# Modulation products in four column quarters of the array, and the square of the decay on ScalarE

## The chip, the cores and the metric

The kernel runs on one core of a Trainium2 chip. The metric is device time in microseconds: the median of three runs before was 2331.62 us (2330.88 to 2336.09). The profiled execution took 2334.22 us in all, and its span, from the first to the last instruction, 2332.4 us.

## The reference, cut to what matters

Two layers of a hybrid mixer are run for 1024 latent and 256 context tokens of 1024 channels. Each layer is modulated by a conditioning vector, one for each of the two token groups:

```python
mod = jnp.dot(jax.nn.silu(cvec), p['w_ada']) + p['b_ada']   # 1024 -> 3072
shift, scale, gate = jnp.split(mod[:, None, :], 3, axis=-1)
h = rmsnorm(x, p['norm_g']) * (1.0 + scale) + shift
...                                   # attention, Hyena and RG-LRU heads from h
a = jnp.exp(log_a)                    # the RG-LRU's decay
b = jnp.sqrt(-jnp.expm1(2.0 * log_a)) * (i * xf)
...
x_new = x + gate * out                # out: the output projection
```

`mod` is a product of two rows (the two conditioning vectors) with a 1024 x 3072 matrix, once a layer, all in float32. `expm1(2 log_a)` comes from the decay: it is a*a - 1.

## The kernel before, in words

Channels lie on the 128 partitions, in eight tiles of 128, and tokens run along the free dimension, in chunks of 512, 512 and 256. Large projections are done with weights and activations split into two float16 halves (`proj`, L680; `out_acc`, L1316), three products for each pair of tiles.

The modulation is done with the conditioning vectors as the stationary operand (128 x 2) and the matrix as the moving one (128 x 512), so that 512 outputs take eight products, one for each tile of the 1024 contracted channels, added up in two partitions of one PSUM tile. A float32 product stands in the trace as two passes. Those two rows of 512 are then copied to SBUF by VectorE, turned by four transposes of TensorE into columns (128 x 2 each), and added to the bias into `modv`. Two generators do this:

- `ada()` makes shift and scale of layer 0 at the start of the program: four rows of 512 (products on L473, copies on L476, transposes on L479). The 16 matrix tiles of 128 x 1024 (`wa`, 512 KB each) are loaded in the order that the string `ORD` gives, mixed with the eight input tiles `xs`. They have eight buffers (tag `h`), so that the second eight wait until the first eight have been multiplied. `ada_in(0)` then makes `sh_t` and `sc_t`, without which the first normalised tile (`make_h`) can't be made. `make_h` also needs `first`, the inverse norm that `FirstSquares` makes on TensorE, ScalarE and VectorE.
- `ada_rest(l, o0)` makes the other rows in steps (products on L499, copies on L502, transposes on L506): two rows of layer 0 (its gate) beside the RG-LRU of layer 0, and six rows of layer 1 beside the output projection of layer 0. Four tiles of 256 KB are loaded in one step (tag `bn`, four buffers, which other lines use too) and multiplied in the next.

`weave` mixes the steps of such generators into a main loop, each at a rate of its own, and so gives the order of the source. The program's order on each engine is not that order to the letter: a list scheduler issues the earliest instruction of the source that it takes to be ready, by its own estimates of durations. At run time every engine's order is fixed. All DMAs are issued in order from SyncE's queue.

In `lru_post`, for each of four channel tiles and two directions in a layer, the decay `a` comes from ScalarE (Exp). GpSimd multiplies it by itself into `a2`, and VectorE uses `a2` in a `scalar_tensor_tensor` that gives a*a - 1 times a factor. Another one, on `ti`, stands just before it on VectorE. Calls to ScalarE show as L155, to VectorE as L149 and L152, and GpSimd's products as L152, since helpers record them.

Of the kernel before, what the change touches and what calls it, by code (L numbers as in the profile page):

```python
# [10 lines left out]
F32 = mybir.dt.float32  # L11
F16 = mybir.dt.float16
AF = mybir.ActivationFunctionType
ALU = mybir.AluOpType
AX = mybir.AxisListType
ADD, SUB, MUL, MAX, MIN = ALU.add, ALU.subtract, ALU.mult, ALU.max, ALU.min

P = 128
# [4 lines left out]
T = NL + NP  # L23
# [5 lines left out]
KT = 8  # L29
# [24 lines left out]
PRM = {}  # L54
# [57 lines left out]
def hybrid_step(ctx, tc, xT, cT, w_ada, w_in, w_out, prm, fpk, w1, w2, w3, decay, ck, cv, wlru,  # L112
# [3 lines left out]
    cp = ctx.enter_context(tc.tile_pool(name="cp", bufs=1))  # L116
# [5 lines left out]
    V, A, G, PE = nc.vector, nc.scalar, nc.gpsimd, nc.tensor  # L122
# [4 lines left out]
    def nm(s):  # L127
        uid[0] += 1
        return f"{s}_{uid[0]}"


    def S(tag, shape=(P, W5), dt=F32):
        return sp.tile(list(shape), dt, tag=tag, name=nm(tag), bufs=BUFS[tag])
# [4 lines left out]
    def B(tag, shape=(P, 512), dt=F32):  # L138
        return S(tag, shape, dt)

    def PS(tag, shape=(P, 512)):
        tag = PTAG[tag]
        return ps.tile(list(shape), F32, tag=tag, name=nm(tag), bufs=PTAG["n" + tag])

    def load(dst, src):
        return nc.sync.dma_start(dst, src)

    def stt(out, a, s, b, o0=MUL, o1=ADD, eng=None):
        return (eng or V).scalar_tensor_tensor(out, a, s, b, o0, o1)  # L149

    def tt(out, a, b, op, eng=None):
        (eng or V).tensor_tensor(out, a, b, op)  # L152

    def act(out, a, f, scale=1.0, bias=0.0):
        A.activation(out, a, f, bias=bias, scale=scale)  # L155
# [30 lines left out]
    modv = cp.tile([P, DEPTH, 24, 2], F32, name="modv")  # L186
# [19 lines left out]
    def pv(l, name, i=0):  # L206
        o, n = PRM[name]
        return pr[:, l, o + i:o + i + 1]
# [247 lines left out]
                    load((Hl, Hp)[kind][l, hf, q], h)  # L456
                    yield

    silu_c = cp.tile([P, KT, 2], F32, name="silu_c")

    def ada():

        sc = silu_c
        th = sm.tile([P, KT, 2], F32, name="th_c")
        act(th, cT_t, AF.Tanh, scale=0.5)
        V.tensor_scalar(th, th, 0.5, 0.5, MUL, ADD)
        tt(sc, th, cT_t, MUL)
        for o in (0, 8):
            p = [PS("m" if o else "s") for _ in range(2)]
            for k in range(KT):  # L470
                wt = wa[o + k]
                for i, pi in enumerate(p):
                    PE.matmul(pi[:2], sc[:, k], wt[:, 512 * i:512 * i + 512], start=(k == 0), stop=(k == KT - 1))  # L473
            for i, pi in enumerate(p):
                row = B("ba")
                V.tensor_copy(row[:2, :512], pi[:2])  # L476
                pt = PS("o")
                for j in range(4):
                    PE.transpose(pt[:, 2 * j:2 * j + 2], row[:2, P * j:P * j + P], ident[:2, :2])  # L479
                q = o + 4 * i  # L480
                b = pr[:, 0, PRM["b_ada"][0] + q:PRM["b_ada"][0] + q + 4]
                tt(modv[:, 0, q:q + 4], pt[:, :8].rearrange("p (a b) -> p a b", b=2),
                   b[:, :, None].to_broadcast([P, 4, 2]), ADD)
            if o:
                ada_in(0)
            yield

    def ada_rest(l, o0=0):

        for o in range(o0, 24, 4):  # L490
            p = PS("s")
            for k0 in range(0, KT, 4):
                raws = []
                for k in range(k0, k0 + 4):
                    raws.append(B("bn"))
                    load(raws[-1], w_ada[l, k, :, P * o:P * o + 512])
                yield
                for k, raw in enumerate(raws, k0):
                    PE.matmul(p[:2], silu_c[:, k], raw, start=(k == 0), stop=(k == KT - 1))  # L499
                yield  # L500
            row = B("bn")
            V.tensor_copy(row[:2, :512], p[:2])  # L502
            yield
            pt = PS("s")
            for j in range(4):
                PE.transpose(pt[:, 2 * j:2 * j + 2], row[:2, P * j:P * j + P], ident[:2, :2])  # L506
            b = pr[:, l, PRM["b_ada"][0] + o:PRM["b_ada"][0] + o + 4]
            tt(modv[:, l, o:o + 4], pt[:, :8].rearrange("p (a b) -> p a b", b=2),
               b[:, :, None].to_broadcast([P, 4, 2]), ADD)
            if o == 12:  # L510
                ada_in(l)
            yield
        V.tensor_scalar(gt_t[:, l], modv[:, l, 16:24], 1.0 / SW, None, MUL)

    def ada_in(l):
        V.tensor_scalar(sh_t[:, l], modv[:, l, 0:8], SH, None, MUL)
        g = pvs(l, "norm_g")

        V.tensor_scalar(sc_t[:, l], modv[:, l, 8:16], 1.0, -0.5 * SH, ADD, MUL)
        tt(sc_t[:, l], sc_t[:, l], g[:, :, None].to_broadcast([P, 8, 2]), MUL)  # L520
# [195 lines left out]
    def conv(u, taps, bias):  # L716

        t = S("a")
        for a, b, o in ((0, NL, 0), (NL, T, GAP - NL)):
            act(t[:, a:b], u[:, a + o:b + o], AF.Identity, scale=taps[0], bias=bias)  # L720
            for j in range(1, len(taps)):
                stt(t[:, a:b], u[:, a + o + j:b + o + j], taps[j], t[:, a:b])
        return t

    def park(i, m):

        for c0, n in CH:
            t = B("ba", (P, 2, 512), F16)
            act(t[:, 0, :n], m[:, c0:c0 + n], AF.Copy)
            tt(t[:, 1, :n], m[:, c0:c0 + n], t[:, 0, :n], SUB, G)  # L730
            load(Md[i, :, :, c0:c0 + n], t[:, :, :n])
# [33 lines left out]
    def lru_post(l, i, out):  # L765
        u, gate = out[i]
        xc = conv(u, [pv(l, "lw", 4 * i + j) for j in range(4)], pv(l, "lb", i))
        wr, wt = B("ld", (P, 4, P)), B("ld", (P, 2, 4, P), F16)
        load(wr, wlru[l, i])
        act(wt[:, 0], wr, AF.Copy, scale=SW)  # L770
        stt(wt[:, 1], wr, SW, wt[:, 0], MUL, SUB)
        x2 = S("a", (P, 2, W5), F16)
        act(x2[:, 0, :T], xc[:, :T], AF.Copy)
        tt(x2[:, 1, :T], xc[:, :T], x2[:, 0, :T], SUB, ENG[XL])
        yield
        st = []
        for d in range(2):
            ta, ti = S("a"), S("a")
            for c0, n in CH:
                for z, dst, bo_ in ((0, ta, 4 * d + i), (1, ti, 8 + 4 * d + i)):  # L780
                    p = PS("s")
                    for j, (a, b) in enumerate(((0, 0), (0, 1), (1, 0))):
                        PE.matmul(p[:, :n], wt[:, a, 2 * d + z], x2[:, b, c0:c0 + n], start=(j == 0), stop=(j == 2))
                    act(dst[:, c0:c0 + n], p[:, :n], AF.Tanh, scale=0.5 / SW, bias=hba[:, l, bo_:bo_ + 1])
                yield
            s_, n_ = lr_sp[:, l, 0, 4 * d + i:4 * d + i + 1], lr_sp[:, l, 1, 4 * d + i:4 * d + i + 1]
            a = S("a")

            act(a[:, :T], ta[:, :T], AF.Exp, scale=s_, bias=s_)
            act(ta[:, :T], ta[:, :T], AF.Tanh, scale=n_, bias=n_)  # L790
            stt(ti[:, :T], ti[:, :T], 1.0, xc[:, :T], ADD, MUL)
            a2 = S("a")
            tt(a2[:, :T], a[:, :T], a[:, :T], MUL, G)
            stt(ta[:, :T], a2[:, :T], 1.0, ta[:, :T], ADD, MUL)
            st.append((a, ta, ti))
            yield
        for d, (a, ta, ti) in enumerate(st):
            act(ta[:, :T], ta[:, :T], AF.Sqrt, scale=0.25)
        ys = []
        for d, (a, ta, ti) in enumerate(st):  # L800
            tt(ti[:, :T], ti[:, :T], ta[:, :T], MUL, ENG[LE[d]])
            h0 = pv(l, "h0", 4 * d + i)
            L, Q = slice(0, NL), slice(NL, T)
            if d:
                L, Q = slice(NL - 1, None, -1), slice(T - 1, NL - 1, -1)
            V.tensor_tensor_scan(ta[:, L], a[:, L], ti[:, L], h0, MUL, ADD)
            V.tensor_tensor_scan(ta[:, Q], a[:, Q], ti[:, Q], 0.0, MUL, ADD)
            e = NL if d else T - 1
            load(newh[l, d, i], ta[:, e:e + 1])
            ys.append(ta)  # L810
            yield
        m = ys[0]
        tt(m[:, :T], ys[0][:, :T], ys[1][:, :T], ADD, ENG[LE[2]])
        stt(m[:, :T], m[:, :T], GS, gate[:, :T], MUL, MUL)
        yield
        park(4 + i, m)
        yield
# [569 lines left out]
    xs, wa = [], []  # L1387
    for c in ORD:
        if c == "x":
            i = len(xs)  # L1390
            xs.append(S("f" if i < 4 else "a"))
            load(xs[i][:, :T], xT[i])
        elif c == "c":
            ident = const("ident", [P, P], ident_in)
            pr = const("pr", [P, DEPTH, NPRM], prm)
            ones = const("ones", [P, P], ones_h)
        else:
            i = len(wa)
# [237 lines left out]
```

## Time and profile before

| | value |
|---|---|
| median of three runs | 2331.62 us |
| profiled execution: time, span | 2334.22 us, 2332.4 us |
| TensorE (PE) busy | 2103.2 us, 90% |
| VectorE (DVE) busy | 1730.1 us, 74% |
| ScalarE (ACT) busy | 1232.3 us, 53% |
| GpSimd (POOL) busy | 806.5 us, 35% |
| mean granted clock of TensorE | 0.967 |

Busy time of TensorE is that of pipelined instructions: in a row of equal matmuls the distance from start to start is shorter than the duration of one, and it is the distance that counts. PEld is the loading of stationary operands, which overlaps the matmuls. "Idle before <-" names what ended the idle time before an instruction. DVE, ACT, POOL and SP stand for VectorE, ScalarE, GpSimd and SyncE.

### The profile page before, as it was taken

To read this page: it belongs to the slowest core of one execution; us is meant where nothing else is said; L and a number is where in the kernel's file an instruction comes from. 1 tells how busy PE (TensorE), PEld (TensorE's weight loads), DVE (VectorE), ACT (ScalarE), POOL (GpSimd) and SP (SyncE) were. 2 spreads that over 40 slices of the span, in tenths; PEclk is the share of its full clock that TensorE was granted. 3 is DMA by queue.
4 is the path that set the end of the run, shared out by engine and by line. 5 is a ranking of instruction groups with operands and counts; after the bars stand their busy time and mean duration, and the time that the engine had idled before them with its cause. 6 is when DMAs were issued, how large, how long until landed. Compare 5 with 4: busy or idle time off the path is not lost. (4 is left out here: it accounts for less than half of the span.)

```text
span 2332.4 us, 38033 instructions
## 1 busy us (share of the span) xinstructions
PE 2103.2 (90%) x14288; PEld 1238.6 (53%) x14288; DVE 1730.1 (74%) x2765; ACT 1232.3 (53%) x2157; POOL 806.5 (35%) x746
## 2 busy tenths in 40 slices
PE   8787889989998999999998899999899898999997
PEld 2344435546544566676444444455555556666674
DVE  6987887487769888875757877766774998777547
ACT  6765755334333477676342677634433427566562
POOL 4332142123503365565212321131440316444450
PEclk9899989999999999999999999999999999999999
DMA  7314215234214432112475122223431334111114
GB/s 272 123 37 123 76 56 133 63 109 133 84 39 137 126 117 67 56 56 93 151 230 178 46 53 43 56 69 93 135 94 55 113 103 148 53 57 57 46 45 153
DMA packets 154696, 226.10 MB, mean 97 GB/s; under 512 B 22148, under 2 KB 74541, under 8 KB 154512
## 3 DMA queue, kind: packets, MB, share of 16 engines
q1 hardware_dynamic: 154512, 223.67, 31.6%
q8 instruction: 112, 1.84, 0.3%
q14 instruction: 72, 0.59, 0.1%
HBM read 170.73 MB, written 49.03 MB: 94 GB/s over the span
## 5 line engine op out<-in xcount | busy, mean ns | idle before, releaser
L680 PE MATMUL acc<-h,wh 128*128 128x512 f16 (+1 forms) x3264 | 864.0, 351 | 38.4 <-DVE f L149 17.1
L680 PE MATMUL acc<-h,wl 128*128 128x512 f16 (+1 forms) x1632 | 571.8, 350 | 0.0
L680 PEld LDWEIGHTS <-wh 128*128 128x128 f16 x3264 | 324.1, 99 | 311.7 <-issue 69.6
L152 POOL TENSOR_TENSOR y<-by,y 128x512 f16<-128x512 f32 x272 | 318.0, 1188 | 229.8 <-issue 138.1
L680 PEld LDWEIGHTS <-wl 128*128 128x128 f16 x1632 | 162.4, 99 | 162.6 <-issue 38.0
L155 ACT ACTIVATE f<-acc 128x512 f32<-128x512 f32 (+1 forms) x204 | 105.2, 519 | 264.9 <-PE acc L680 263.1
L1316 PE MATMUL acc<-h,wh 128*128 128x512 f16 (+1 forms) x768 | 199.3, 344 | 0.0
L155 ACT ACTIVATE by<-s 128x512 f32<-128x512 f32 x208 | 135.1, 649 | 110.3 <-PE s L1197 109.5
L1170 DVE TENSOR_REDUCE mxl<-m 128x1 f32<-128x512 f32 x288 | 186.3, 680 | 8.7 <-PE m L1169 8.6
L149 DVE SCALAR_TENSOR_TENSOR a<-f,pr,a 128x1024 f32<-128x1024 f32 (+1 forms) x144 | 147.9, 1045 | 60.1 <-ACT a L155 57.7
L152 DVE TENSOR_TENSOR y<-by,y 128x512 f16<-128x512 f32 x128 | 121.2, 947 | 66.5 <-ACT y L155 62.9
L155 ACT ACTIVATE wh<-wr 128x512 f16<-128x512 f32 x184 | 113.4, 626 | 94.8 <-PE acc L1316 47.8
L1223 PE MATMUL o<-va,y 128*128 128x130 f16 x1600 | 160.4, 220 | 1.8 <-DVE f L149 1.7
L1224 PE MATMUL o<-va,y 128*128 128x65 f16 x1600 | 155.3, 193 | 7.1 <-POOL y L152 6.0
L1316 PEld LDWEIGHTS <-wh 128*128 128x128 f16 x1152 | 108.8, 98 | 88.9 <-issue 10.6
L1224 PEld LDWEIGHTS <-y 128*128 128x128 f16 x1600 | 140.9, 98 | 23.2 <-POOL y L152 8.8
L1223 PEld LDWEIGHTS <-y 128*128 128x128 f16 x1600 | 142.2, 97 | 12.7 <-issue 7.8
L370 PE MATMUL m<-y,ld 128*128 128x256 f16 x960 | 122.7, 277 | 26.4 <-ACT y L155 14.9
L152 DVE TENSOR_TENSOR y<-y,y 128x256 f32<-128x256 f32 (+4 forms) x160 | 127.6, 826 | 13.0 <-ACT y L155 13.0
L149 DVE SCALAR_TENSOR_TENSOR wl<-wr,wh 128x512 f16<-128x512 f32 x168 | 130.2, 784 | 8.7 <-ACT wh L155 7.8
L155 ACT ACTIVATE y<-s 128x512 f16<-128x512 f32 x208 | 136.0, 654 | 0.0
L1169 PE MATMUL m<-k,a 128*128 128x512 f16 x288 | 110.8, 385 | 24.9 <-DVE mxl L1170 23.7
(209 smaller groups left out, 4147.3 us busy)
## 6 DMA issues: line engine op xcount, KB each, us to landing
wr<-in_w_in SPq DMA_DIRECT2D x136, 256.0 KB
bn<-in_w_ada SPq DMA_DIRECT2D x64, 256.0 KB
wr<-in_w_out SPq DMA_DIRECT2D x48, 256.0 KB
ld<-in_fhl SPq DMA_DIRECT2D x56, 192.0 KB
h<-Md SPq DMA_DIRECT2D x16, 640.0 KB
h<-in_w_ada SPq DMA_DIRECT2D x16, 512.0 KB
Md<-ba SPq DMA_DIRECT2D x32, 256.0 KB
Hl<-by SPq DMA_DIRECT2D x32, 256.0 KB
```

What stands on the lines that cost most here:

```text
L149: return (eng or V).scalar_tensor_tensor(out, a, s, b, o0, o1)
L152: (eng or V).tensor_tensor(out, a, b, op)
L155: A.activation(out, a, f, bias=bias, scale=scale)
L370: PE.matmul(x[:, o], cn[:, y, c], hl[:, z, g], start=(k == 0 and j == 0), stop=(k == 1 and j == 2))
L680: PE.matmul(acc[:, :n], w[k // 4][wi][:, P * (k % 4):P * (k % 4) + P], h[k][:, x, c0:c0 + n], start=(k == 0 and j == 0), stop=(k == KT - 1 ...
L1169: PE.matmul(p, lhs, k1[g][:, 512 * c:512 * c + 512], start=True, stop=True)
L1170: V.tensor_reduce(mxl[:, 8 * e + qt, c:c + 1], p, AX.X, MAX)
L1223: PE.matmul(o[:, qt], p[:, 0], va[g][:, s0 + s], start=(s == 0), stop=False)
L1224: PE.matmul(o[:, qt, 0], p[:, 1], va[g][:, s0 + s, 0], start=False, stop=(s == ns - 1))
L1316: PE.matmul(acc[:, :n], wt[:, cs], mix[k][:, x, c0:c0 + n], start=(i == 0 and j == 0), stop=(i == len(ks) - 1 and j == 2))
```

## The change

The stationary operand `silu_c` gets 32 columns for each contraction tile, two with the vectors and thirty of zeros. The product of contraction tile k is put into the column quarter k mod 4 of the array (`tile_position`), and so into 32 partitions of its own of the PSUM tile, where tiles k and k + 4 add up. The row of 128 partitions is copied whole, and instead of four transposes four products with a 0/1 matrix `pick` (128 x 2, made from the identity) both turn it and add the four quarters. In `ada()` the products of four contraction tiles stand together in the source, first those of one PSUM tile and then those of the other. In `ada_rest` the step between the copy and the transposes is gone. In `lru_post` the square of the decay is an activation of ScalarE.

```diff
--- before.py
+++ after.py
@@ -456,11 +456,28 @@
                     load((Hl, Hp)[kind][l, hf, q], h)
                     yield
 
-    silu_c = cp.tile([P, KT, 2], F32, name="silu_c")
+    silu_c = cp.tile([P, KT, 32], F32, name="silu_c")
+    pick = cp.tile([P, 2], F32, name="pick")
+
+    def ada_row(p, row, pt, l, q):
+
+        V.tensor_copy(row, p)
+        for j in range(4):
+            PE.matmul(pt[:, 2 * j:2 * j + 2], row[:, P * j:P * j + P], pick, start=True, stop=True)
+        b = pr[:, l, PRM["b_ada"][0] + q:PRM["b_ada"][0] + q + 4]
+        tt(modv[:, l, q:q + 4], pt[:, :8].rearrange("p (a b) -> p a b", b=2),
+           b[:, :, None].to_broadcast([P, 4, 2]), ADD)
+
+    def ada_mm(p, w, k):
+
+        j = 32 * (k % 4)
+        PE.matmul(p[j:j + 32], silu_c[:, k], w, start=(k < 4), stop=(k >= KT - 4), tile_position=(0, j))
 
     def ada():
 
-        sc = silu_c
+        sc = silu_c[:, :, 0:2]
+        V.memset(silu_c, 0.0)
+        V.tensor_reduce(pick, ident.rearrange("p (j b) -> p b j", j=4)[:, 0:2], AX.X, ADD)
         th = sm.tile([P, KT, 2], F32, name="th_c")
         act(th, cT_t, AF.Tanh, scale=0.5)
         V.tensor_scalar(th, th, 0.5, 0.5, MUL, ADD)
@@ -468,19 +485,13 @@
         for o in (0, 8):
             p = [PS("m" if o else "s") for _ in range(2)]
             for k in range(KT):
-                wt = wa[o + k]
+                if k % 4 < 3:
+                    continue
                 for i, pi in enumerate(p):
-                    PE.matmul(pi[:2], sc[:, k], wt[:, 512 * i:512 * i + 512], start=(k == 0), stop=(k == KT - 1))
+                    for k4 in range(k - 3, k + 1):
+                        ada_mm(pi, wa[o + k4][:, 512 * i:512 * i + 512], k4)
             for i, pi in enumerate(p):
-                row = B("ba")
-                V.tensor_copy(row[:2, :512], pi[:2])
-                pt = PS("o")
-                for j in range(4):
-                    PE.transpose(pt[:, 2 * j:2 * j + 2], row[:2, P * j:P * j + P], ident[:2, :2])
-                q = o + 4 * i
-                b = pr[:, 0, PRM["b_ada"][0] + q:PRM["b_ada"][0] + q + 4]
-                tt(modv[:, 0, q:q + 4], pt[:, :8].rearrange("p (a b) -> p a b", b=2),
-                   b[:, :, None].to_broadcast([P, 4, 2]), ADD)
+                ada_row(pi, B("ba")[:, :512], PS("o"), 0, o + 4 * i)
             if o:
                 ada_in(0)
             yield
@@ -496,17 +507,9 @@
                     load(raws[-1], w_ada[l, k, :, P * o:P * o + 512])
                 yield
                 for k, raw in enumerate(raws, k0):
-                    PE.matmul(p[:2], silu_c[:, k], raw, start=(k == 0), stop=(k == KT - 1))
+                    ada_mm(p, raw, k)
                 yield
-            row = B("bn")
-            V.tensor_copy(row[:2, :512], p[:2])
-            yield
-            pt = PS("s")
-            for j in range(4):
-                PE.transpose(pt[:, 2 * j:2 * j + 2], row[:2, P * j:P * j + P], ident[:2, :2])
-            b = pr[:, l, PRM["b_ada"][0] + o:PRM["b_ada"][0] + o + 4]
-            tt(modv[:, l, o:o + 4], pt[:, :8].rearrange("p (a b) -> p a b", b=2),
-               b[:, :, None].to_broadcast([P, 4, 2]), ADD)
+            ada_row(p, B("bn"), PS("s"), l, o)
             if o == 12:
                 ada_in(l)
             yield
@@ -790,7 +793,7 @@
             act(ta[:, :T], ta[:, :T], AF.Tanh, scale=n_, bias=n_)
             stt(ti[:, :T], ti[:, :T], 1.0, xc[:, :T], ADD, MUL)
             a2 = S("a")
-            tt(a2[:, :T], a[:, :T], a[:, :T], MUL, G)
+            act(a2[:, :T], a[:, :T], AF.Square)
             stt(ta[:, :T], a2[:, :T], 1.0, ta[:, :T], ADD, MUL)
             st.append((a, ta, ti))
             yield
```

## Rows read from the trace of the kernel before

**Rows 1.** Page, part 1: busy us (share of the span) xinstructions

```profile
PE 2103.2 (90%) x14288; PEld 1238.6 (53%) x14288; DVE 1730.1 (74%) x2765; ACT 1232.3 (53%) x2157; POOL 806.5 (35%) x746
```

**Rows 2.** Busy time by stretch, us from the start; columns in the first line

```profile
core 0: us, PE busy (x) PEld busy (x) DVE busy (x) ACT busy (x) POOL busy (x), PEclk, DMA share, GB/s
14.00:64.00 50.00, 47.43 (x111) 12.15 (x110) 36.68 (x59) 34.55 (x61) 19.07 (x19) 0.97 0.66 252
...
130.00:420.00 290.00, 243.36 (x1283) 128.32 (x1283) 229.92 (x250) 167.92 (x236) 82.80 (x68) 0.91 0.32 83
1080.00:1250.00 170.00, 156.50 (x866) 73.68 (x863) 111.88 (x173) 61.77 (x110) 42.93 (x25) 0.99 0.55 178
1300.00:1530.00 230.00, 206.28 (x1053) 105.70 (x1052) 175.97 (x162) 155.56 (x226) 53.54 (x62) 0.94 0.21 45
```

**Rows 3.** Readers of silu_c: count, min/median/max ns, first and last start, form

```profile
L499 PEld LDWEIGHTS s<-bn,silu_c x128: 80/84/129, 166.3 to 1240.3; 128*2 128x2 f32 x128
L499 PE MATMUL s<-bn,silu_c x128: 591/592/1061, 166.3 to 1240.8; 128*2 128x512 f32 x128
...
L473 PE MATMUL s<-h,silu_c x32: 591/592/1057, 14.0 to 43.2; 128*2 128x512 f32 x32
...
L473 PE MATMUL m<-h,silu_c x32: 591/592/593, 44.0 to 62.6; 128*2 128x512 f32 x32
```

**Rows 4.** PE timeline, 54 to 69 us: start, length, operation, count, [idle before]

```profile
54.49 8.74 PE L473 MATMUL m<-h,silu_c 128*2 128x512 f32 x20
63.16 0.41 PE L479 MATMUL o<-ident,ba 2*128 2x2 f32 x4
...
68.13 1.01 PE L680 MATMUL acc<-h,wh 128*128 128x512 f16 x2 [3.65 <-ACT h L155]
```

**Rows 5.** DVE timeline, 57 to 66 us

```profile
57.28 0.69 DVE L149 SCALAR_TENSOR_TENSOR by<-bn,bn 128x512 f32<-128x512 f32 x1
...
65.90 0.16 DVE L152 TENSOR_TENSOR sc_t<-sc_t,pr 128x16 f32<-128x16 f32 x1
```

**Rows 6.** PE timeline, 1102 to 1107 us

```profile
1102.62 0.38 PE L1316 MATMUL acc<-a,wl 128*128 128x512 f16 x1
1102.92 3.59 PE L499 MATMUL s<-bn,silu_c 128*2 128x512 f32 x8
1106.45 0.39 PE L1316 MATMUL acc<-h,wh 128*128 128x256 f16 x2
```

**Rows 7.** Line L579 (ones product of FirstSquares): weight loads, columns as in Rows 3

```profile
L579 PEld LDWEIGHTS acc<-bn,ones x24: 186/190/337, 27.3 to 54.0; 128*128 128x128 f32 x24
```

**Rows 8.** Waits, PEld, 1080 to 1250 us: us in total, times, longest

```profile
PEld s L499 <- DMA bn<-in_w_ada: 11.9, 16, 2.3
```

**Rows 9.** Timelines of POOL and DVE at 212 us, of DVE at 1364

```profile
212.20 2.32 POOL L152 TENSOR_TENSOR a<-a 128x1280 f32<-128x1280 f32 x1 [10.22 <-ACT a L155]
...
212.51 4.75 DVE L149 SCALAR_TENSOR_TENSOR a<-a,a 128x1280 f32<-128x1280 f32 x2 [3.84 <-ACT a L155]
...
1364.62 1.47 DVE L149 SCALAR_TENSOR_TENSOR a<-a,a 128x1280 f32<-128x1280 f32 x1
```

**Rows 10.** DVE groups, 130:420 and 1300:1560: busy us, mean ns | idle before

```profile
L149 DVE SCALAR_TENSOR_TENSOR a<-a,a 128x1280 f32<-128x1280 f32 x16 | 33.4, 2099 | 13.4 <-ACT a L155 8.9 <-POOL a L152 4.4
...
L149 DVE SCALAR_TENSOR_TENSOR a<-a,a 128x1280 f32<-128x1280 f32 x16 | 33.3, 2095 | 33.6 <-ACT a L155 33.6
```

**Rows 11.** ACT timeline, 35 and 212 us

```profile
35.96 0.21 ACT L155 ACTIVATE e<-e 128x8 f32<-128x8 f32 x1
36.07 1.44 ACT L155 ACTIVATE bn<-f 128x512 f32<-128x512 f32 x3
...
212.38 1.44 ACT L155 ACTIVATE a<-a,lr_sp 128x1280 f32<-128x1280 f32 x1
```

**Rows 12.** ACT groups, 130 to 420 us, columns as in Rows 10

```profile
L155 ACT ACTIVATE a<-a,lr_sp 128x1280 f32<-128x1280 f32 x16 | 23.2, 1452 | 0.2
```

**Rows 13.** Waits, PE, 130 to 420 us

```profile
PE s L783 <- ACT a L155: 14.8, 5, 4.8
```

## Prediction

> **What bounds the kernel now.** I read the page first: TensorE is busy for 90% of the span and no other engine for more than 74% [rows 1]. Then busy time by stretch, where the change lies: TensorE is busy for 95% of 14 to 64 us, 84% of 130 to 420 (layer 0's RG-LRU), 92% of 1080 to 1250 (layer 0's output projection) and 90% of 1300 to 1530 (layer 1's RG-LRU) [rows 2]. So time taken from TensorE is mostly time taken from the end, save where a chain of small steps on VectorE and ScalarE is late as well, as in the RG-LRU. Last I read the lines themselves, the timelines round them, and the waits.
>
> **What the products cost now.** Lines L473 and L499 are 64 and 128 passes, for 32 and 64 products: two passes each [rows 3]. Twenty of them in a row take 8.74 us and one lasts 0.592 [rows 3, 4], so they stand (8.74 - 0.59) / 19 = 0.429 us apart. That makes 64 x 0.429 = 27.5 us at the start and 128 x 0.429 = 54.9 us later, 82 us of TensorE. The 128 passes of L499 lie in 28 blocks in the PE timeline: nine of 8 passes, two of 6, five of 4, twelve of 2. Two of the 8s and three of the 4s are among the seven blocks before 400 us, the rest among the 21 of 1080 to 1250.
>
> **How far quarters overlap.** No row shows a product in a part of the array. The bounds are no overlap (0.429 us a pass, as now) and four at a time. I take the middle, and say why: the two passes of one product write the same quarter and have to follow each other, but the first pass of the next product can run beside the second of the last, if TensorE starts them in the order of the program. A block of n passes then takes n/2 + 1 places of 0.429 us instead of n. Blocks of 8 win 1.29 us, of 6 0.86, of 4 0.43, of 2 nothing.
>
> A block also pays for going in and out. Now L1316 to L499 takes 0.30 us from start to start and the last of the eight passes to the next L1316 0.53 (1102.92 + 7 x 0.429 = 1105.92, then 1106.45), where L1316's own distance is 0.59 - 0.38 = 0.21 (two in a row against one) and that of L499 0.429 [rows 6]: some 0.09 and 0.10 us over the pace. The Trainium skill (TensorEngine Tiling (Array Packing), Key Properties) says that going from one tiling mode to another drains the engine; this speaks against blocks between 128-column products. Its draining has no price there; by the rule the whole rest of a pass, 0.592 - 0.429 = 0.16 us, would be lost at either end, where I take the 0.09 again, and the sum would be 5 us worse. I take 0.18 us more for each block, with bounds of 0 and 0.33.
>
> **The rows that follow.** Copies stay: 512 elements on each partition. Four transposes take 0.41 us [rows 4]. Four products with `pick` are float32 products, so eight passes, with 128 x 128 stationary. Bounds for a row: the same 0.41 (nothing more), and eight weight loads of 0.19 one after another [rows 7], 1.52, so 1.1 more. I take twice the transposes, 0.4 more, for 12 rows.
>
> **Start, four rows.** The sources of one group stand together, so I take four groups of 16 passes: each wins 7 x 0.429 = 3.0 us, 12 in all. Against it 4 x 0.4 = 1.6 and eight blocks x 0.18 = 1.4: 9 us of TensorE. The end of the stage is `sc_t`, finished at 66.06; the other thing that `make_h` needs, the inverse norm of the first 512 tokens, is done at 57.97 [rows 5]. So 8.1 us is what can go; then the norm is late. The second eight matrix tiles come free as soon as the first are multiplied, not later than now. The memset of `silu_c` and the making of `pick` are small instructions in front of 60 us of other work. I take **-8**, bounds +3 (no overlap, rows and blocks paid) and -9.
>
> **Layer 0's gate, two rows.** -2 x 1.29 - 3 x 0.43 = -3.9, seven blocks +1.3, rows +0.8: -1.8; at a stage of 84% busy I take **-1**.
>
> **Layer 1's rows, six.** -(7 x 1.29 + 2 x 0.86 + 2 x 0.43) = -11.6, 21 blocks +3.8, rows +2.4: -5.4; at 92% busy **-5**. The step that is gone brings each row's loads forward by one in six, past other DMAs in SyncE's queue, and the copy is now followed at once by what waits for it: TensorE's queue stands behind VectorE's copy unless the scheduler finds other work for it, which it did between steps before. The passes already wait 11.9 us for `w_ada` there, 16 times [rows 8]. What that eats is a rival below.
>
> **The square.** GpSimd's product runs for 2.32 us, and the `scalar_tensor_tensor` on `ti` that VectorE starts 0.3 us behind it, and the next one, take 4.75 us together, where one alone takes 1.47 [rows 9]: VectorE gets on only when GpSimd is done. Over the 16 of them in each layer the mean is 2.10 us, so (2.099 - 1.474) x 16 = 10.0 us of VectorE's time a layer [rows 10], 20 in all. ScalarE gets 16 x 1.45 = 23 us [rows 12]. It needs no new table: squares of `FirstSquares` stand right behind an Exp without a load between [rows 11]. In the chain the square would now follow the Tanh (212.38 + 1.44) and end near 215.3; the second of VectorE's pair began at 212.51 + 4.75 - 1.47 = 215.79 [rows 9, 11]. So 0.5 us is won 16 times, 8 us, while ScalarE's next gate is 1.45 us later. Bounds: -20 (all of VectorE's stall) and +23 (all of ScalarE's time). VectorE is 79% and ScalarE 58% busy there in layer 0, 77% and 68% in layer 1 [rows 2], so relief is worth a little more than load. I take **-4**.
>
> **Sum.** -8 - 1 - 5 - 4 = -18. The profiled execution took 2334.2, so 2316.2; the median of the runs is 2.6 lower, so **2314**, with 2303 to 2326 as this case's own range: blocks move it by up to 6 us at their bounds, rows by 5 and 8, the square by 8 within the inner half of its own, and I allow 12 together.
>
> **Rivals.**
>
> *Quarters take turns.* If a pass in another quarter waits for the one before it, nothing is won, and rows and blocks are paid: start +3, layer 0 +2, layer 1 +6, square -4: +7. If in addition each pass waits for its own weight load (0.084 us [rows 3]; now hidden, since passes stand at 0.429), 192 x 0.084 = 16 more. Between them +15: 2347, range 2337 to 2355. It decides when passes inside a block stand 0.43 us or more apart. For it: no row shows overlap, and the scheduler leaves twelve blocks of one product, which can't overlap at all. Against it: the passes write separate partitions.
>
> *Four at a time.* The products of a block run beside each other, each with its two passes one after the other, so that every block takes two places. Layer 1 wins 7 x 2.57 + 2 x 1.7 + 2 x 0.86 = 23 instead of 11.6, layer 0 2 x 2.57 + 3 x 0.86 = 7.7 instead of 3.9; the start can't win more than the norm leaves. With blocks, rows and busy shares as above -8 - 5 - 15 - 4 = -32: 2300. The Trainium skill (TensorE: Matmul & The Clock Gate, Measured speedup vs the span model) has 2.38 times for three column tiles, which would bring it here; no run here shows it yet. Against it: two passes of one product share a quarter.
>
> *The square sits in ScalarE's queue.* TensorE already waits 14.8 us for ScalarE's gates in layer 0 [rows 13]. If half of the 23 us comes out there, +12 replaces -4: -2, 2330.
>
> *The gain turns into waiting for `w_ada`*: layer 1's -5 goes, 2319.
>
> **Chances.** Forecast 0.48, waiting for `w_ada` 0.07, four at a time 0.13, turns 0.18, the square 0.14. About 0.2% (4.7 us) is what a measurement of this kernel can tell from no change. Faster: the first three less 0.03 of the forecast's upper tail, 0.65. Same: that tail and most of the square's case, 0.15. Slower: turns and the rest of it, 0.20. The range from 2294 to 2342 holds the forecast, most of "four at a time" and the lower part of "turns".
>
> **What would show it.** Starts of passes inside a block of the changed products: 0.215 us apart on average is the forecast, 0.43 or more turns, 0.11 four at a time. `sc_t` should be ready near 57 us and the first L680 near 60, not at 68.13 [rows 4]. VectorE's group of 1280 should be at 1.48 us a piece. The prediction is wrong if the new schedule breaks the groups of four into single products, or if L680's first start doesn't move.

## The result: some 1% faster, most of it from the square

The changed kernel takes 2304.5 us (2300.1 to 2309.7, four runs) against 2331.6 before: ratio 0.9885, 95% interval 0.9867 to 0.9904, or 27 us less. A second set of runs (e6) gave 0.9904 (0.9887 to 0.9922). The forecast was 2314. The profiled execution has a span of 2299.8 us against 2332.4.

The page's first part, and the stretches that answer to [rows 1, 2], of the changed kernel (its stages lie 12 to 32 us earlier, so the windows are moved, and the last three are shorter):

```profile
PE 2067.4 (90%) x14336; PEld 1238.8 (54%) x14336; DVE 1704.0 (74%) x2767; ACT 1246.6 (54%) x2173; POOL 761.1 (33%) x730
```

```profile
14.00:64.00 50.00, 38.48 (x131) 13.88 (x131) 37.94 (x62) 34.36 (x61) 17.43 (x19) 0.94 0.66 252
118.00:405.00 287.00, 242.63 (x1335) 132.88 (x1333) 229.12 (x293) 181.72 (x258) 69.45 (x61) 0.92 0.34 87
1062.00:1205.00 143.00, 138.75 (x819) 69.02 (x817) 92.00 (x152) 50.37 (x91) 27.14 (x19) 1.00 0.58 192
1290.00:1500.00 210.00, 193.58 (x1022) 101.19 (x1021) 149.76 (x150) 154.49 (x216) 26.79 (x53) 0.97 0.22 46
```

At the start TensorE is now less busy (38.5 of 50 us, 47.4 before), and GpSimd has lost 45 us over the whole. To see where the end moved, I follow the matmuls that write `acc`, without the ones products: the projections' (L680 and L1316 before) and some of attention's (L1196, L1197). There are 7392 of them in either trace, and compare the start of the n-th. Inside a stage the two orders differ; between stages they agree, and only those places stand here (us). The last four columns are e1, e2, e5 and e7 of the experiments below:

```
n       stage that ends there          before   change  square  quarters  dead product  fours
0       start                            68.1     -1.2    -0.7      -1.3          -1.1   +0.7
1050    layer 0's RG-LRU                429.0    -13.8   -13.9      -1.8          -6.3  -14.6
3000    layer 0's attention            1043.2    -18.7   -13.5      -1.4          -8.3  -16.1
3900    output projection, first of
        layer 1's projections          1361.2    -27.0   -13.2      -7.9         -13.3  -31.3
4500    layer 1's RG-LRU               1513.8    -31.9   -19.0     -10.3         -13.3  -37.6
end                                    2332.4    -32.6   -18.4      -8.7         -14.3  -36.4
```

The start gave 1 us, layer 0's RG-LRU 13, layer 0's output projection 8, layer 1's RG-LRU 5; the 5 us between 429 and 1043 can't be told from chance. The changed kernel traced once more (e6) has -0.8, -13.4, -15.0, -21.1, -26.5 and -26.2 in the same six rows, so a stage read from one trace is good to some 3 us, and the end to 6.

**The products.** The readers of `silu_c` and a block of eight passes, of the changed kernel (columns as in [rows 3, 4]):

```profile
L474 PEld LDWEIGHTS s<-bn,silu_c x128: 106/109/155, 159.1 to 1198.7; 128*32 128x32 f32 x128
L474 PE MATMUL s<-bn,silu_c x128: 592/617/1061, 159.1 to 1199.2; 128*32 128x512 f32 x128
```

```profile
325.83 1.06 PE L474 MATMUL s<-bn,silu_c 128*32 128x512 f32 x8
326.82 0.28 PE L683 MATMUL acc<-h,wh 128*128 128x256 f16 x1
```

Eight passes in 1.06 us, where eight took 3.59 [rows 6]. Their starts in the trace, from the first, are 0, 6, 13, 20, 453, 460, 466 and 473 ns: the first passes of four products side by side, then the four second passes. But few blocks are so full. The same timeline at 1130 us shows what most of them look like, and what a row's turning costs (its first line):

```profile
1086.12 0.95 PE L466 MATMUL s<-pick,bn 128*128 128x2 f32 x8
...
1129.94 0.38 PE L1319 MATMUL acc<-a,wh 128*128 128x512 f16 x1
1130.26 1.05 PE L474 MATMUL s<-bn,silu_c 128*32 128x512 f32 x4
1131.24 0.39 PE L1319 MATMUL acc<-a,wh 128*128 128x512 f16 x1
...
1131.99 1.05 PE L474 MATMUL s<-bn,silu_c 128*32 128x512 f32 x2
...
1133.94 1.05 PE L474 MATMUL s<-bn,silu_c 128*32 128x512 f32 x2
```

Two passes take as long as eight: 1.05 us. Over the trace the 192 passes lie in blocks of 2 (24 blocks), 4 (12), 6 (2), 8 (6), 16 and 20; counted from first to last start plus one place of 0.43 us, they hold TensorE for 53.7 us, against 86.8 before.

**The square.** VectorE's groups on 128 x 1280 in the two RG-LRU stages, of the changed kernel, that answer to [rows 10]:

```profile
L149 DVE SCALAR_TENSOR_TENSOR a<-a,a 128x1280 f32<-128x1280 f32 x16 | 24.1, 1508 | 8.8 <-ACT a L155 8.8
```

```profile
L149 DVE SCALAR_TENSOR_TENSOR a<-a,a 128x1280 f32<-128x1280 f32 x16 | 23.8, 1488 | 36.5 <-ACT a L155 36.4
```

The means have gone from 2.10 to 1.51 and 1.49 us: (2.099 - 1.508 + 2.095 - 1.488) x 16 = 19.2 us of VectorE's time are free.

**The start.** VectorE's and TensorE's timelines of the changed kernel, that answer to [rows 4, 5]:

```profile
56.77 0.69 DVE L149 SCALAR_TENSOR_TENSOR by<-bn,bn 128x512 f32<-128x512 f32 x1
57.38 1.28 DVE L464 COPY ba<-m 128x512 f32<-128x512 f32 x2
59.21 0.17 DVE L152 TENSOR_TENSOR modv<-o,pr 128x8 f32<-128x8 f32 x1 [0.55 <-PE o L466]
...
61.20 0.17 DVE L522 TENSOR_SCALAR sc_t<-modv 128x16 f32<-128x16 f32 x1
...
61.62 0.16 DVE L152 TENSOR_TENSOR sc_t<-sc_t,pr 128x16 f32<-128x16 f32 x1
61.70 0.68 DVE L149 SCALAR_TENSOR_TENSOR by<-bn,bn 128x512 f32<-128x512 f32 x1
62.30 0.41 DVE L152 TENSOR_TENSOR bn<-bn,bn 128x256 f32<-128x256 f32 x1
62.64 0.68 DVE L149 SCALAR_TENSOR_TENSOR wl<-wr,wh 128x512 f16<-128x512 f32 x1
...
63.58 1.89 DVE L149 SCALAR_TENSOR_TENSOR wl<-wr,wh 128x512 f16<-128x512 f32 x3
65.39 2.07 DVE L149 SCALAR_TENSOR_TENSOR f<-f,sc_t,by 128x512 f32<-128x512 f32 x3
```

```profile
66.94 1.01 PE L683 MATMUL acc<-h,wh 128*128 128x512 f16 x2 [6.45 <-ACT h L155]
```

`sc_t` is ready at 61.78 instead of 66.06, but `make_h`'s first instruction comes at 65.39, behind the norms of the other chunks and four weight halves. Before, VectorE had done those while it waited for `sc_t`.

### The profile page after: what moved, and what is told of

It is laid out like the page before. It is cut to its first block, busy times and chain, and to the rows that moved or that the text cites. A ratio compares the mean times of both kernels' runs of the same rounds, so it can differ in the third digit from the quotient of the medians.

```text
span 2299.8 us, 38100 instructions
## 1 busy us (share of the span) xinstructions
PE 2067.4 (90%) x14336; PEld 1238.8 (54%) x14336; DVE 1704.0 (74%) x2767; ACT 1246.6 (54%) x2173; POOL 761.1 (33%) x730
## 5 line engine op out<-in xcount | busy, mean ns | idle before, releaser
L683 PE MATMUL acc<-h,wh 128*128 128x512 f16 (+1 forms) x3264 | 857.2, 349 | 38.4 <-DVE h L152 11.5
L683 PE MATMUL acc<-h,wl 128*128 128x512 f16 (+1 forms) x1632 | 568.7, 348 | 0.0
L149 DVE SCALAR_TENSOR_TENSOR a<-f,pr,a 128x1024 f32<-128x1024 f32 (+1 forms) x144 | 141.2, 1002 | 62.2 <-ACT a L155 59.9
L149 DVE SCALAR_TENSOR_TENSOR wl<-wr,wh 128x512 f16<-128x512 f32 x168 | 128.6, 779 | 15.6 <-ACT wh L155 14.5
L1319 PE MATMUL acc<-h,wl 128*128 128x512 f16 (+1 forms) x384 | 132.4, 345 | 0.0
```

Of the source, the lines that this page charges most:

```text
L683: PE.matmul(acc[:, :n], w[k // 4][wi][:, P * (k % 4):P * (k % 4) + P], h[k][:, x, c0:c0 + n], start=(k == 0 and j == 0), stop=(k == KT - 1 ...
L1319: PE.matmul(acc[:, :n], wt[:, cs], mix[k][:, x, c0:c0 + n], start=(i == 0 and j == 0), stop=(i == len(ks) - 1 and j == 2))
```

## The experiments

All times are medians; the ratio is to the kernel before on the same chip, with its 95% interval. Chips differ by up to 0.5% in the kernel before (2328.2 to 2339.0), so ratios are compared, and the us of the last column are (1 - ratio) x 2331.6.

```
run                              us       ratio (interval)          us of gain
changed kernel                   2304.5   0.9885 (0.9867, 0.9904)   26.8
e6  changed kernel again         2308.4   0.9904 (0.9887, 0.9922)   22.4
e1  square alone                 2315.8   0.9935 (0.9912, 0.9958)   15.2
e2  quarters alone               2323.2   0.9963 (0.9949, 0.9976)    8.6
e3  square on VectorE            2317.7   0.9938 (0.9914, 0.9961)   14.5
e5  dead product on GpSimd       2317.6   0.9933 (0.9912, 0.9954)   15.6
e7  fours together               2296.8   0.9854 (0.9839, 0.9870)   34.0
e8  first weights on GpSimd      2305.4   0.9893 (0.9875, 0.9912)   24.9
e9  e7 and e8                    2302.1   0.9884 (0.9864, 0.9903)   27.0
e10 fours in ada_rest alone      2299.1   0.9862 (0.9842, 0.9882)   32.2
e11 step kept                    2309.4   0.9904 (0.9886, 0.9922)   22.4
e12 start undone                 2303.1   0.9884 (0.9865, 0.9902)   27.0
e13 start undone, fours in rest  2301.6   0.9840 (0.9823, 0.9857)   37.3
```

The two measurements of the changed kernel have a mean of 24.6 us; the experiments are set against that. The interval of a gain is some 3 to 5 us to either side.

The mean granted clock of TensorE, as a share of full speed, differs between the kernels too. Over the runs of one chip it is 0.970 before, 0.972 in e1 and 0.966 in e2, e3 and e5; on another 0.971 before, 0.967 in the changed kernel (e6) and 0.965 in e7; on a third 0.970 before, 0.964 in e10, 0.966 in e11 and 0.971 in e12; on e13's 0.969 before and 0.968. So each kernel with quarters in `ada()` has a lower clock than the kernel before beside it, by 0.003 or more, and those without them (e1, e12, e13) lie between 0.001 below it and 0.002 above. Within the kernel before, on the third chip, 2325.09 us went with 0.973 and 2338.75 with 0.966; a line through the eleven runs there gives 1.5 us for each 0.001, so that 0.004 would be some 6 us, an estimate. The quarters may thus win more than their 8.6 us and lose part of it to the clock; no run holds the clock fixed, so this is not shown.

### Which half brings it: e1 and e2

e1 is the kernel before with one line changed, e2 the changed kernel with that line taken back:

```diff
-            tt(a2[:, :T], a[:, :T], a[:, :T], MUL, G)
+            act(a2[:, :T], a[:, :T], AF.Square)
```

> The kernel before with the square of the decay on ScalarE and nothing else. Measured for the whole change: 2304.5 against 2331.6, -27. Theory A (the square is worth more than I put on it: VectorE no longer waits for GpSimd in both RG-LRU stages, where the traces part by 13 us in layer 0 and 5 us in layer 1): 2312 to 2320. Theory B (the square is worth the 4 us of the prediction and the quarters the rest): 2326 to 2330. Rival (ScalarE's 23 us come out): above 2332.

> The changed kernel with the square back on GpSimd. Theory A: the quarters are worth 8 to 15 us, so 2317 to 2324. Theory B: 23 us, so 2306 to 2310. In both the products' passes lie as in the changed kernel: four first passes 7 ns apart where four products stand together, and the first L680 near 67 us.

The square alone gives 15.2 us and the quarters alone 8.6, 23.8 together, so the two add up. Theory A holds, theory B falls. In the table of stages the square's column has the whole of layer 0's RG-LRU (-13.9) and 6 us in layer 1's; the quarters' column has next to nothing until the output projection.

### What the square takes away: e3 and e5

```diff
-            act(a2[:, :T], a[:, :T], AF.Square)
+            tt(a2[:, :T], a[:, :T], a[:, :T], MUL)                  # e3, VectorE
```

```diff
             act(a2[:, :T], a[:, :T], AF.Square)
+            tt(k1[0][:, :T], a[:, :T], a[:, :T], MUL, G)            # e5
```

> The changed kernel with the square on VectorE (1280 elements, 1.48 us as its other products of that size) instead of ScalarE. It takes GpSimd away as the change does, but loads VectorE and not ScalarE. If the gain of the square is VectorE's freedom from GpSimd (20 us of VectorE's time), VectorE pays 16 x 1.48 = 24 us back and this is no better than the square on GpSimd: 8 to 16 us above the changed kernel. If the gain is GpSimd's late result in the chain (a2 ready late), this is as fast as the changed kernel within 5 us or faster.

> The changed kernel with a product a*a of 1280 elements on GpSimd beside ScalarE's square, written to a key buffer that is filled anew later; nothing waits for it. If VectorE being held by GpSimd is what the square's move takes away, the scalar_tensor_tensor on ti is stretched to 3.4 us again and most of the square's gain goes: 8 to 14 us above the changed kernel. If the gain is the chain (a2 earlier), it stays within 4 us of the changed kernel.

Both lose some 10 us of the changed kernel's 24.6. In e5 the chain is that of the changed kernel, ScalarE has the same work and nobody reads GpSimd's result; only GpSimd's work is back, and with it VectorE's long instructions. Its groups in the two stages, and one of them beside GpSimd's dead product of layer 1, with that product:

```profile
L149 DVE SCALAR_TENSOR_TENSOR a<-a,a 128x1280 f32<-128x1280 f32 x16 | 29.1, 1822 | 9.2 <-ACT a L155 9.2
```

```profile
L149 DVE SCALAR_TENSOR_TENSOR a<-a,a 128x1280 f32<-128x1280 f32 x16 | 33.0, 2080 | 32.2 <-ACT a L155 32.2
```

```profile
1398.89 3.54 DVE L149 SCALAR_TENSOR_TENSOR a<-a,a 128x1280 f32<-128x1280 f32 x1
...
1403.54 1.48 DVE L149 SCALAR_TENSOR_TENSOR a<-a,a 128x1280 f32<-128x1280 f32 x1
```

```profile
1398.69 2.39 POOL L152 TENSOR_TENSOR k<-a 128x1280 f16<-128x1280 f32 x1 [9.51 <-ACT a L155]
```

That is (1.822 - 1.508 + 2.080 - 1.488) x 16 = 14.5 us more of VectorE's time, and 9 us more at the end. So GpSimd holding VectorE accounts for 9 of the 16 us that the square brings to the quarters (24.6 - 8.6). It is not all of it: e5 is 5.7 us faster than e2 on the same chip (2317.6 against 2323.2; the ranges of their runs, 2313.7 to 2319.9 and 2319.4 to 2327.3, hardly overlap), though VectorE's group of layer 0 is held as long in e2. What e2 has and e5 has not is VectorE's wait for `a2` itself, as in [rows 10]:

```profile
L149 DVE SCALAR_TENSOR_TENSOR a<-a,a 128x1280 f32<-128x1280 f32 x16 | 27.9, 1758 | 8.6 <-ACT a L155 4.8 <-POOL a L152 3.8
```

So an earlier `a2` seems to have a share as well; it is read from this wait and was not tested alone. e3, without GpSimd but with 16 x 1.48 = 24 us of squares on VectorE, ends where e5 does. That fits the 8 to 16 us expected of it, but it is 5.5 us faster than e2, where I had expected it to be no better.

### What the quarters leave: e7, e10 and e13

```diff
+    def ada_four(p, ws, k0):
+        last = ada_mm(p, ws[3], k0 + 3)
+        with tc.issue_after(last.ins):
+            for k in range(3):
+                ada_mm(p, ws[k], k0 + k)
...
-                for k, raw in enumerate(raws, k0):
-                    ada_mm(p, raw, k)
+                ada_four(p, raws, k0)
```

e7 does this in `ada()` too, e10 in `ada_rest` alone, and e13 in `ada_rest` with `ada()` as it was before the change.

> The changed kernel, but the product of the last tile of a group of four is issued first and the other three are queued right behind it, so that the four stand together. In the changed kernel's trace 37 of the 43 blocks after the start hold one or two products: fifteen blocks of 4 passes and twenty-one of 2. If the time of L474's passes on TensorE comes out at the end, blocks of 8 take 2 x 0.43 us in place of (two or three blocks) 4 to 6 times 0.43: about 26 us of passes go to 14, so 6 to 10 us off the changed kernel, 2295 to 2300. Rival (waiting for the last of four tiles costs what the overlap gives, since the passes already wait for w_ada there): no change, within 3 us. A plain loss of over 5 us would say that the order round them matters more than either.

> Fours together in ada_rest alone; ada() as in the changed kernel. With fours together everywhere the first L680 started 1.9 us later than in the changed kernel (the last tile of a group is waited for), while the output projection of layer 0 gained some 9 us. If the two add up, the start's 2 us come back: 2294 to 2297. Rival (the start's 2 us don't reach the end): within 2 us of the kernel with fours everywhere, 2296.8.

> ada() as before the change, and in ada_rest fours together, with the square on ScalarE. If the start of the change is worth nothing (the kernel with the start undone took 2303, the changed one 2305 to 2308) and fours together in ada_rest are worth 9 us, this is as fast as the kernel with fours everywhere, 2294 to 2299. If the start's quarters count once the rest is better, 2300 to 2305.

The count in e7's expectation is off: 36 blocks stand after the start, and 29 of them hold one or two products, nine of 4 passes and twenty of 2. e7 is 9.4 us better than the changed kernel's mean (11.5 on the same chip), about what was expected. Its products hold TensorE for 26.9 us instead of 53.7 (13.0 instead of 30.7 in the output projection). TensorE's timeline of e7 at 1131 us:

```profile
1129.91 0.38 PE L1324 MATMUL acc<-a,wh 128*128 128x512 f16 x1
1131.15 1.06 PE L474 MATMUL s<-bn,silu_c 128*32 128x512 f32 x8 [0.86 <-DMA bn<-in_w_ada]
1132.15 0.39 PE L1324 MATMUL acc<-a,wh 128*128 128x512 f16 x1
```

It waits 0.86 us for the last of the four tiles and still wins, since three blocks of 1.05 us go. From 1060 to 1220 us TensorE's matmuls wait 6.2 us for `w_ada` instead of 1.0, against 17.7 us less of passes. e10's and e13's gains of 32.2 and 37.3 us have intervals that overlap e7's: the start's quarters add nothing that can be told. (e13 ran on a chip where the kernel before takes 2339.0 us; its ratio would be 2294 us on the first chip, the value expected if the start is worth nothing.) My expectation that the start's 2 us would come back in e10 is neither borne out nor refuted.

### The start: e8, e9 and e12

e8 splits the first four weight tiles on GpSimd, e12 makes `ada()` with two columns and transposes as before, e9 is e7 with e8:

```diff
-                    v = [split_w(w_in[l, TIDX[n], :, 512 * i:512 * i + 512], WENG[n[0]]) for i in range(2)]
+                    v = [split_w(w_in[l, TIDX[n], :, 512 * i:512 * i + 512],
+                                 "G" if l == 0 and n in ("lx0", "gl0") else WENG[n[0]]) for i in range(2)]
```

> The changed kernel with ada() as it was: two-column products, four transposes. The prediction had the start at -8, which would make this 8 us slower than the changed kernel, 2313 to 2316. The trace has its first L680 only 1.2 us earlier than before, since VectorE's list is late in place of sc_t: by that, 0 to 3 us slower than the changed kernel.

> The changed kernel with the first four weight tiles split by GpSimd instead of VectorE. In the changed kernel sc_t is ready 4.4 us earlier than before, but VectorE then does four weight halves and the other chunks' norms before the first tile of make_h, and the first L680 starts only 1.2 us earlier. If VectorE's order is what held the start's gain back, four halves of 0.68 us go from it: the first projection starts 2 to 3 us earlier and the time falls by 1 to 3 us. Rival: GpSimd holds VectorE as it does in the RG-LRU, and nothing is won (0 to +4).

> Fours together and the first four weight tiles split by GpSimd: the sum of the two, 2293 to 2300 if both theories hold, 2300 to 2310 if neither does.

e12 is no slower than the changed kernel (27.0 against 24.6 us of gain), and its first projection starts at 67.3 us against 66.9: the start's quarters are worth nothing that shows at the end, where the prediction had 8 us. With the start undone the mean granted clock is 0.971, against 0.966 in e11 on the same chip, so part of what the quarters win there may go to the clock; that is open. e8 took the four weight halves off VectorE and got 0.3 us for it, nothing that shows. Its VectorE and GpSimd timelines show why:

```profile
61.37 1.12 DVE L522 TENSOR_SCALAR sc_t<-modv 128x16 f32<-128x16 f32 x1
...
63.84 1.37 DVE L152 TENSOR_TENSOR bn<-bn,bn 128x256 f32<-128x256 f32 x1
65.13 0.74 DVE L149 SCALAR_TENSOR_TENSOR f<-f,sc_t,by 128x512 f32<-128x512 f32 x1
```

```profile
60.88 1.58 POOL L152 TENSOR_TENSOR wl<-wr,wh 128x512 f16<-128x512 f32 x1
62.43 0.86 POOL L626 TENSOR_SCALAR wr<-wr 128x512 f32<-128x512 f32 x1
63.26 1.66 POOL L152 TENSOR_TENSOR wl<-wr,wh 128x512 f16<-128x512 f32 x1
```

An instruction on 16 columns, 0.17 us in the changed kernel, lasts 1.12, until GpSimd's product is done; 256 columns 1.37 instead of 0.41. The rival holds: GpSimd gives VectorE's time back by holding it. e9, at 2302.1, missed its 2293 to 2300 and is 5 us behind e7 on the same chip. Its first projection starts 1.2 us later than e7's (70.0 against 68.8); the rest is not explained.

### The removed step: e11

```diff
-            ada_row(p, B("bn"), PS("s"), l, o)
+            row = B("bn")
+            V.tensor_copy(row, p)
+            yield
+            ada_turn(row, PS("s"), l, o)      # the products with pick and the add
```

> The changed kernel with the step between the copy of a row and its products kept in ada_rest. If the removed step made TensorE wait behind VectorE's copy (the price that I left to a rival), this is faster by up to 8 rows x 1 us. If the scheduler finds other products for it, as L1319 stands before L466 without idle time in the changed kernel's trace, no change: within 4 us of the changed kernel.

A gain of 22.4 us, against 24.6 for the changed kernel's mean, with intervals that overlap: the step costs and gives nothing that shows.

## Why the prediction came out as it did

The forecast's direction and its range held. Two terms were far off, in opposite directions, and the sum hides that: that the range held is luck. By the prediction's own signs it failed in part: 20 of the 36 blocks after the start hold a single product, and L680's first start moved by 1.2 us where 8 were forecast.

**The square, -4 forecast, -15 measured.** The mechanism was read rightly: VectorE is held until GpSimd is done [rows 9, 10]. The failing step is "so relief is worth a little more than load". I set VectorE's 20 us against ScalarE's 23 us as if both came out alike. They did not: of the 14.5 us of VectorE's time that e5 gives back to GpSimd, 9 come out at the end, and of ScalarE's 23 us nothing that shows, since e5 has them and is still faster than e2. What I had read from the one chain at 212 us (0.5 us won 16 times) may stand for the 6 us between e2 and e5. Left out was the rest: VectorE's freed time goes to whatever is next in its list. That ScalarE's share could be carried could have been read from [rows 2]: it was busy for 58 and 68% there against VectorE's 79 and 77%. In the changed kernel it is 63 and 74% (181.7 of 287 and 154.5 of 210 us) against 80 and 71%. The rival in which the square sits in ScalarE's queue did not happen: TensorE's wait for ScalarE's gates in layer 0 fell from 14.8 us [rows 13] to 6.8, and there are 49 table loads in either trace:

```profile
PE s L786 <- ACT a L155: 6.8, 5, 4.4
```

**The start, -8 forecast, nothing measured.** TensorE did win its time: the passes hold it for 17.0 us instead of 29.6. But `sc_t`, forecast near 57 us, was ready only at 61.78, still behind the norm at 57.46, and `make_h` did not start then either. Of the 7.9 us between the norm and `make_h` VectorE is idle for 1.1; the rest are the copies and adds that make `sc_t`, the other chunks' norms and four weight halves. The norms and weight halves it used to do while it waited for `sc_t`. The term should have been the idle time of VectorE before `make_h`, not the distance from norm to `sc_t`: before, it was idle for some 1.1 us between the norm at 57.97 and `make_h` at 66.59, about the 1.2 us by which L680 moved. VectorE's timeline of the kernel before:

```profile
58.79 1.96 DVE L152 TENSOR_TENSOR bn<-bn,bn 128x512 f32<-128x512 f32 x4 [0.81 <-ACT bn L155]
...
63.27 0.68 DVE L476 COPY ba<-m 2x512 f32<-2x512 f32 x1 [0.18 <-PE m L473]
...
66.59 2.06 DVE L149 SCALAR_TENSOR_TENSOR f<-f,sc_t,by 128x512 f32<-128x512 f32 x3
```

**The quarters' overlap, pairs forecast, fours measured.** The assumption that failed is that the second pass of one product runs beside the first pass of the next, so that a product more costs a place more; here all first passes go side by side, and then all second ones. The page TensorE: Matmul & The Clock Gate of the Trainium skill (Measured speedup vs the span model) gives 2.38 times for three column tiles; here a block of four products is 3.4 times as fast (3.59 / 1.06 us), so that rule led the right way and the rival "four at a time" is right for such a block. It is right for the six blocks of eight passes and the two longer ones at the start only: the scheduler issues each product when it takes its tile to be there. I took the blocks of before as fixed; in the output projection they went from seven of 8, two of 6 and two of 4 passes, beside 2s, to one of 8, two of 6, nine of 4 and twenty of 2. Two errors met, the overlap taken too small and the blocks too full: -6 was forecast for `ada_rest`, and the quarters alone gave 8.6. e7 shows what fuller blocks give. Nor was a stage's busy share a price: in e2 the passes of layer 0's RG-LRU hold TensorE for 5.4 us instead of 14.9 and that stage, 84% busy, gained 0.5 us, while 11 us less in the output projection, 92% busy, brought 6.5.

**Going in and out, 0.18 us a block forecast, nothing measured.** Into a block takes 0.31 us and out of it 0.53 in the changed kernel's trace, 0.30 and 0.53 before. The distance before rested on two L1316 in a row, a row that stands here, from TensorE's timeline of the kernel before:

```profile
1102.18 0.59 PE L1316 MATMUL acc<-a,wh 128*128 128x512 f16 x2
```

The Trainium skill's rule of draining (TensorEngine Tiling (Array Packing), Key Properties) shows no price here beyond what going between these products already cost before.

**A row's turning, +0.4 forecast:** 0.95 us for the eight passes (1.05 at the start) against 0.41, so +0.5 to +0.6. **Waiting for `w_ada`**: the passes' loads wait 4.5 us instead of 11.9 [rows 8], so that rival did not happen:

```profile
PEld s L474 <- DMA bn<-in_w_ada: 4.5, 6, 1.2
```

## What to carry to other kernels

An instruction of GpSimd that runs beside VectorE is not a free lane: look for VectorE's instructions that last longer than their kin of the same form, and price the difference at more than half its length (9 of 14.5 us here) where VectorE is busy for three quarters of the stage. Products that are to overlap have to stand together in the issued order, and the scheduler's order pulled them apart here; tying them to the last operand's arrival won as much again (9 us) as the quarters as they were first issued (8.6). When a late operand is made earlier, count what the consumer's engine has been doing while it waited, since it still has to be done.

## What the runs showed of the hardware that I had not expected

Four float32 products in four column quarters of the array start 7 ns apart, each second pass 453 ns after its first, and a pass is hardly longer (0.617 against 0.592 us) than one with two columns before. A switch between quarters and the whole array cost no more (0.31 us in, 0.53 out) than one between the two-column float32 products and the float16 ones had before (0.30 and 0.53). VectorE's smallest instructions are held as the large ones are: 128 x 16 elements lasted 1.12 us instead of 0.17 beside a product of GpSimd. And the hold goes both ways. In the kernel before, the VectorE instruction at 1364.62 took 1.47 us but was not alone, it came first [rows 9]. GpSimd's product, started 0.23 us behind it, lasted 3.42 us instead of 2.32, and VectorE's next, of 512 columns, 2.81 instead of 0.67:

```profile
1364.85 3.42 POOL L152 TENSOR_TENSOR a<-a 128x1280 f32<-128x1280 f32 x1 [8.69 <-ACT a L155]
```

```profile
1366.00 2.81 DVE L149 SCALAR_TENSOR_TENSOR wl<-wr,wh 128x512 f16<-128x512 f32 x1
```
